# The third down-projection weight pair gets a place of its own and is loaded with the first two; the up stage's pools in another order

## The chip, the cores and the metric

The kernel is one program on one core of one Trainium2 chip. The metric is the device time of one execution in microseconds (us). A core has a matrix engine (TensorE, PE in the profile), a vector engine (DVE), a scalar engine (ACT), GpSimd (POOL) and SyncE (SP, which here only issues transfers). They run in parallel from their own instruction lists and wait for one another by semaphores. Operands lie in SBUF, an on-chip memory of 128 partitions; matmul results go to the eight banks of PSUM, and ACT and DVE carry them from there to SBUF.

## The reference

One inference step of a one-layer encoder trunk, all in float32: 1024 frames of a new stream and 64 frames of a running one (1088 rows), model width 1024.

```python
xn = rmsnorm(x, g)
proj = xn @ w_in                      # conv inputs B, C, h; q, k, v; two merge gates
ya = (B * causal_conv3(C * h)) @ w_cout
yb = band_attend(q, k, v, rel_bias) @ w_attn_out
x = x + (sigmoid(ga) * ya + sigmoid(gb) * yb) @ w_out
h = silu(xn2 @ w_ff1) * (xn2 @ w_ff3)  # xn2 = rmsnorm(x, g_ffn), inner width 2816
x = x + h @ w_ff2
y = rmsnorm(x, g_final)               # and the rolled caches
```

## The kernel before

**Arithmetic.** Each float32 operand is split into a high part (a rounded copy, a CAST by ACT, line 121) and a low part (the operand less the high part, a TENSOR_TENSOR by DVE, line 122). A product takes three matmuls: high by high, high by low, low by high. The large products are also done by Strassen-Winograd's scheme, in seven half-sized products for eight. They are always done in the order `STEPS = [1, 2, 6, 7, 5, 4, 3]`; steps 1, 2, 4 and 3 use quarters of the operands as they are, steps 6, 7 and 5 use sums of quarters.

**Stages**, by the profiled execution: norm, transposes and V (to 110 us), the rest of the input projection (to 340), gates and attention (to about 590), the merge of the two branches (`ya`, `yb`; to 692.6), the output product (`wo`, to 807, with the second norm's transposes between), the up stage and the down stage.

**The up stage** (to 1264.5) has 22 units of about 21 us, in pairs a0, b0 … a10, b10 (w_ff1 and w_ff3, 128 inner columns by two each). The moving operand of step p is the transposed activation, in a tile `mg` for steps 1, 2, 4, 3 and a tile `tt` for steps 6, 7, 5; the weights (`wha`, `whb`, `wla`, `wlb`) are stationary. A step is 24 matmuls of 272 columns. Results of the pair p go as `sa`, `sb` through SiLU and a product to `hq` buffers (three of them) and by a GpSimd-issued store to device memory (`h_d`), seven stores of 512 KB for each pair.

**The down stage** (1264.5 to 1506) multiplies by w_ff2. Its 22 rows of 128 are taken as 11 pairs `kp`, in four blocks of 2, 3, 3, 3 pairs. In a block, for each half g of the frames and each step p, PE does three matmuls for each pair and each of two frame tiles (12 in a row in the first block, 18 in a block of three; 132 for a step over the whole stage), with `ht` (read back from `h_d`) stationary and `ring` moving, 512 columns each. `ring1` to `ring7` hold the split weights, one tile for each step: `ring1`, `ring2`, `ring4`, `ring3` in the place of `mg`, `ring6`, `ring7`, `ring5` in the place of `tt` (pool `tpool`). PSUM results named A, B, D are copied (ACT, line 1518) or added (DVE, line 1520) to accumulators `acc`. After each block and half, the 64 running frames are done by `ys` matmuls.

The class `Down` stands for one pair: creating it loads its 1 MB of weights into a tile `w2r` (line 1304), and its seven `prep` steps split it into the rings (on DVE also subtractions, line 1319, in place or to `sf`). Tile `w2r` comes from `rpool`, two buffers of 8 KB per partition that nearly all weight loads of the kernel share (tag `raw`). So the load of pair kp waits until the last split of pair kp − 2 has read its buffer. Pairs 0 and 1 are created in the last up unit and prepared while it runs. Pairs 2, 3, 4 are created while block 0 runs:

```python
# last up unit, before
for kp in blocks[0]:
    W2[kp] = Down(kp)
ahead = [(W2[kp], {}) for kp in blocks[0]] + [(Refill(), {})]
...
# down stage, block b, half g: nk are the pairs of the next block
for n, kp in enumerate(nk):
    at = {0: 0, 1: 4 if first else 7, 2: 7}[n]
    for st in range(len(STEPS)):
        if (at + st) // 7 == g:
            todo.setdefault((at + st) % 7, []).append((kp, st))
    if at // 7 == g and at % 7 == 0:
        W2[kp] = Down(kp)
```

**What sets the order.** The program text fixes what depends on what; a scheduler then lists the instructions of each engine by its own estimates. So a load that is created elsewhere moves the splits and the copies around it on ACT and DVE. An instruction that waits holds all those behind it on its engine. The same scheduler decides where SP's loads stand.

**Where tiles lie.** Pools that are opened one after another are stacked in SBUF. Offsets in bytes per partition, from the sizes of the pools: scratch of the GpSimd-issued transfers 16384, constants 704, `rpool` 16384; so `tpool` starts at 33472, with `tt6`/`ring6` there, `tt7`/`ring7` at 50880, `tt5`/`ring5` at 68288. Each of these is a multiple of 64. `mg` and `ring1`, `ring2`, `ring4`, `ring3` start at 159712 and on, and `ht` and the stationary weights from 122848 on, each 32 above a multiple of 64. In the rows of the order below, a name ends with a running number, ours to tell tiles apart; the digits ahead of it are the pair, tile or frame.

Of the kernel before, what the change touches and what calls it, by code (L numbers as in the profile page):

```python
# [8 lines left out]
F32 = mybir.dt.float32  # L9
# [6 lines left out]
P = 128  # L16
D = 1024
# [47 lines left out]
def encoder_kernel(ctx: ExitStack, tc: tile.TileContext, ins, outs):  # L65
    nc = tc.nc
# [12 lines left out]
    rpool = ctx.enter_context(tc.tile_pool(name="rpool", bufs=2, reuse_waits="tile"))  # L79
# [94 lines left out]
    class Unit:  # L174
        def __init__(self, src, nm):
            self.nm = nm
            self.raw = rpool.tile([P, KD, 2 * P], F32, tag="raw", name=f"raw{nm}")
            nc.sync.dma_start(self.raw, src.rearrange("(k p) n -> p k n", p=P))
            self.w = {}
# [850 lines left out]
    pg_stack.close()  # L1030


    tpool = ctx.enter_context(tc.tile_pool(name="tpool", bufs=1, reuse_waits="tile"))
    up_stack = ExitStack()
    psA = up_stack.enter_context(tc.tile_pool(name="psA", bufs=2, space=PSUM, reuse_waits="tile"))
    hp0 = ctx.enter_context(tc.tile_pool(name="hp0", bufs=1, reuse_waits="tile"))

    tt = three_sums(tpool, "tt")
    ax = mg.t
# [247 lines left out]
    def refill():  # L1287

        while len(hts) < len(loads_h) and held[0] + len(loads_h[len(hts)][0]) <= 16:
            held[0] += len(loads_h[len(hts)][0])  # L1290
            h_load(*loads_h[len(hts)])
# [6 lines left out]
    class Down:  # L1298


        def __init__(self, kp):
            self.kp = kp
            self.raw = rpool.tile([P, 2, D], F32, tag="raw", name=f"w2r{kp}")
            nc.sync.dma_start(
                self.raw, ins["w_ff2"][0][2 * kp * P : 2 * (kp + 1) * P].rearrange("(r p) n -> p r n", p=P)
            )
            self.w = {}
# [58 lines left out]
    blocks = []  # L1366
# [3 lines left out]
    W2 = {}  # L1370

    def up_unit(n):
        l, p = names[n]
        return Unit(ins["w_ff1" if l == "a" else "w_ff3"][0][:, 2 * p * P : 2 * (p + 1) * P], f"{l}{p}")

    def up_run(n, unit, ahead):
        l, p = names[n]
        return run(unit, operands, bank2, snap2, (gate_done if l == "a" else hidden_done)(p), ahead)
# [26 lines left out]
    for n in range(1, len(names)):  # L1405
        if n + 1 < len(names):
            unit = up_unit(n + 1)
            ahead = [(unit, {2: (0, 1, 2)} if n == 1 else {})]
        else:
            for kp in blocks[0]:  # L1410
                W2[kp] = Down(kp)
            ahead = [(W2[kp], {}) for kp in blocks[0]] + [(Refill(), {})]
            refill()
        if n == 1:
            nxt += ahead
            r = r1
        else:
            r = up_run(n, this, ahead)
        for _ in r:
            pass  # L1420
        this = unit
# [8 lines left out]
    bufs = {(dp, "acc"): 1, (hp, "snap"): 3, (hp, "sa"): 4, (hp0, "snap"): 1, (hp0, "sa"): 1}  # L1430
    for n, (i, d) in enumerate(order):
        if n < len(homes):
            pool, tag = homes[n]
# [28 lines left out]
    for b, ks in enumerate(blocks):  # L1462
        first, final = b == 0, b == len(blocks) - 1
        nk = blocks[b + 1] if not final else []
        for g in range(2):
# [4 lines left out]
            for n, kp in enumerate(nk):  # L1470
                at = {0: 0, 1: 4 if first else 7, 2: 7}[n]
                for st in range(len(STEPS)):
                    if (at + st) // 7 == g:
                        todo.setdefault((at + st) % 7, []).append((kp, st))
                if at // 7 == g and at % 7 == 0:
                    W2[kp] = Down(kp)
            if final:
                xr = []
                for i in (2 * g, 2 * g + 1):
                    raw = rpool.tile([P, 2, D], F32, tag="raw", name=f"x1r{i}")  # L1480
# [13 lines left out]
            for si, js in turns:  # L1494
                p, ht = STEPS[si], hts[base + si]
                key = {1: "A", 6: "A", 5: "A", 3: "A", 2: "B", 7: "D", 4: "D"}[p]
                for j in js:
                    i = 2 * g + j
                    if (key, j) not in ps:
                        ps[key, j] = psD.tile(  # L1500
                            [P, 512], F32, tag="A" if key == "A" else "BD", name=f"{key}{b}_{i}",
                            bufs=2 if key == "A" else 4,
# [88 lines left out]
```

## Time and profile before

| | |
|---|---|
| time before | 1516.06 us, median of 3 runs (1512.9 to 1516.81) |
| span of the profiled execution, first to last instruction | 1513.8 us |
| PE busy | 1476.9 us, 98% of the span |
| DVE, ACT, POOL busy | 981.2 (65%), 682.7 (45%), 128.7 (9%) |
| granted TensorE clock | full in nearly every slice |
| PE between 1284.57 and 1295.9 (start of the down stage) | 4.95 us idle in four waits |
| tail after PE's last matmul | about 8 us |

The profiled execution's own time is known as this span; what lies around the span isn't given apart. The span stands 2.3 us below the median and inside the range of the three runs. In the rows of the profile a line's first number is the start in us, the second how long it is busy; brackets give the idle time ahead and what ended it.

### The profile page before, as it was taken

How to read it: one execution, taken by the hardware profiler on the slowest of the kernel's cores; microseconds unless marked ns; L12 is line 12 of the kernel's file. 1: busy time of each engine (PE TensorE's matmuls, PEld its weight loads, DVE VectorE, ACT ScalarE, POOL GpSimd, SP SyncE). 2: the span in 40 equal slices, each digit the busy share in tenths (PEclk: the TensorE clock that was granted, in tenths of full speed). 3: DMA queues.
4: the chain of work that ended last, by engine and by line, in shares of the span. 5: the costliest groups of instructions: out<-in, count | busy, mean ns of one | idle time of the engine just before them, and what ended most of it. 6: DMA issues, size and time to landing. Idle time of an engine off the chain costs nothing.

```text
span 1513.8 us, 26451 instructions
## 1 busy us (share of the span) xinstructions
PE 1476.9 (98%) x10178; PEld 1381.1 (91%) x10178; DVE 981.2 (65%) x1843; ACT 682.7 (45%) x1397; POOL 128.7 (9%) x236
## 2 busy tenths in 40 slices
PE   7999999999999999999999999999999999999997
PEld 5799999999999999998889999999999998788886
DVE  6886465642776752763489667666666668857576
ACT  6654433333776752542256444444444445402123
POOL 1210010001111121000100011100001011000000
PEclk9999999999999999999999999999999999999999
DMA  7597524168676529554432434443334449667675
GB/s 233 181 305 245 184 78 135 57 187 234 181 186 176 151 82 293 164 167 145 140 126 77 143 134 152 144 148 120 117 142 157 143 177 317 234 221 235 222 259 202
DMA packets 167518, 264.73 MB, mean 175 GB/s; under 512 B 19008, under 2 KB 103168, under 8 KB 167264
## 3 DMA queue, kind: packets, MB, share of 16 engines
q1 hardware_dynamic: 146736, 198.23, 42.2%
q0 software_dynamic: 19504, 62.71, 11.4%
q10 hardware_dynamic: 1152, 2.10, 0.4%
q8 instruction: 80, 1.31, 0.4%
q14 instruction: 46, 0.38, 0.1%
HBM read 171.06 MB, written 91.92 MB: 174 GB/s over the span
## 4 chain that ended last, share of the span: by engine, by line
PE 79%; DMA 8%; DVE 6%; ACT 3%; issue 3%; SPq 1%; POOL 0%; ACTq 0%; POOLq 0%; DVEq 0%
PE Aa L238 9%; PE Ab L238 9%; PE A L1508 7%; PE Da L238 4%; PE Db L238 4%; PE D L1508 3%; PE Bb L238 2%; PE Ba L238 2%; PE B L1508 2%; PE wo L1066 2%; PE wo L1068 2%; PE wo L1067 2%; PE t L903 2%; PE Ak L238 2%; PE g L300 2%
## 5 line engine op out<-in xcount | busy, mean ns | idle before, releaser
L1508 PE MATMUL A<-ring,ht 128*128 128x512 f32 x528 | 126.6, 393 | 3.6 <-ACT acc L1518 1.9
L1508 PEld LDWEIGHTS A<-ring,ht 128*128 128x128 f32 x528 | 98.8, 188 | 27.2 <-ACT acc L1518 3.2
L300 PE MATMUL g<-xn,whp 128*128 128x272 f32 x384 | 113.2, 295 | 0.0
L301 PE MATMUL g<-xn,whp 128*128 128x272 f32 x384 | 112.0, 292 | 0.0
L302 PE MATMUL g<-xn,wlp 128*128 128x272 f32 x384 | 111.6, 291 | 0.0
L121 ACT CAST ring<-w2r 128x512 fp32r<-128x512 f32 (+1 forms) x78 | 43.4, 587 | 105.7 <-PE A L1508 52.6
L121 ACT CAST hq<-sa 128x512 fp32r<-128x512 f32 x77 | 47.7, 619 | 86.4 <-DVE sa L1239 56.6
L814 DVE CUSTOM_DVE_ANT_0 p<-s,bb 128x640 f32<-128x640 f32 (+5 forms) x72 | 47.5, 661 | 45.5 <-DMA bb<-bias_d 28.6
L1227 POOL DMA_DIRECT2D h_d<-hq x77 | 40.9, 532 | 416.5 <-DVE hq L122 242.1
L122 DVE TENSOR_TENSOR hq<-sa,hq 128x512 fp32r<-128x512 f32 x77 | 53.1, 690 | 33.4 <-ACT hq L121 33.3
L300 PEld LDWEIGHTS g<-xn,whp 128*128 128x128 f32 x384 | 72.6, 189 | 1.0
L302 PEld LDWEIGHTS g<-xn,wlp 128*128 128x128 f32 x384 | 72.6, 189 | 0.5
L301 PEld LDWEIGHTS g<-xn,whp 128*128 128x128 f32 x384 | 72.7, 189 | 0.3
L1508 PE MATMUL D<-ring,ht 128*128 128x512 f32 x264 | 63.9, 393 | 1.3 <-ACT acc L1518 1.3
L122 DVE TENSOR_TENSOR wla<-rawa,wha 128x512 fp32r<-128x512 f32 x56 | 38.5, 687 | 40.5 <-ACT wha L121 40.5
L238 PE MATMUL Aa<-tt,wha 128*128 128x272 f32 x352 | 59.1, 289 | 2.5 <-ACT tt L121 2.5
L1508 PEld LDWEIGHTS D<-ring,ht 128*128 128x128 f32 x264 | 49.5, 188 | 13.1 <-ACT acc L1518 1.8
L122 DVE TENSOR_TENSOR ring<-w2r,ring 128x512 fp32r<-128x512 f32 (+1 forms) x78 | 49.0, 647 | 14.4 <-ACT ring L121 14.2
L238 PE MATMUL Ab<-mg,whb 128*128 128x272 f32 x352 | 58.4, 288 | 0.0
L238 PE MATMUL Aa<-mg,wha 128*128 128x272 f32 x352 | 58.3, 288 | 0.0
L238 PE MATMUL Ab<-tt,whb 128*128 128x272 f32 x352 | 58.2, 287 | 0.0
L121 ACT CAST wha<-rawa 128x512 fp32r<-128x512 f32 x56 | 34.8, 621 | 51.3 <-PE Ab L238 35.3
(519 smaller groups left out, 4368.2 us busy)
## 6 DMA issues: line engine op xcount, KB each, us to landing
h_d<-hq POOLq DMA_DIRECT2D x77, 512.0 KB, 3.5
ht<-h_d SPq DMA_DIRECT2D x154, 256.0 KB, 3.7
rawa<-in_w_ff SPq DMA_DIRECT2D x11, 1024.0 KB, 5.9
rawb<-in_w_ff SPq DMA_DIRECT2D x11, 1024.0 KB, 5.4
w2r<-in_w_ff SPq DMA_DIRECT2D x11, 1024.0 KB, 5.8
qd<-q_d SPq DMA_DIRECT2D x32, 272.0 KB, 4.7
rawp<-in_w_in SPq DMA_DIRECT2D x6, 1024.0 KB, 5.9
u_d<-scr SPq DMA_DIRECT2D x8, 544.0 KB, 4.6
```

Source lines behind the costliest of these rows:

```text
L121: act.copy(hi, src)
L122: vec.tensor_tensor(lo, src, hi.bitcast(F32), op=ALU.subtract)
L238: mm(t[:, j, :HN], w[:, k, :], x[p][:, l, k, j * HN : (j + 1) * HN], start=p in (1, 2, 7) and k == 0 and n == 0, stop=k == 3 and n == 2, s ...
L300: mm(out, a, p, start=k == 0, stop=False)
L301: mm(out, a, q, start=False, stop=False)
L302: mm(out, b, p, start=False, stop=k == kt - 1)
L814: vec.tensor_tensor_reduce(out=s if len(ps.shape) == 2 else s.rearrange("p (a b) -> p a b", a=2), in0=ps, in1=bias if len(ps.shape) == 2 e ...
L903: nc.tensor.transpose(tp[:, i * P : (i + 1) * P], s[:, i * P : (i + 1) * P], ident)
L1066: mm(ps, x(k, 0), wh, start=f, stop=False)
L1067: mm(ps, x(k, 0), wl, start=False, stop=False)
L1227: nc.gpsimd.dma_start(h_d[p, c - 1], hq.rearrange("p i l t -> p (i l t)").bitcast(F32))
L1508: mm(t, ht[k][:, j, x], w[:, l], start=p in (1, 2, 7) and k == 0 and n == 0, stop=k == len(ks) - 1 and n == 2, skip_group_check=p in (6, 5 ...
```

## The change

Three things are changed. The pool `hp0` and two new pools are opened ahead of `tpool`: `early`, with one 8 KB tile, and `lead`, with one tile of 32 bytes that nothing reads or writes. The raw weights of pair 2 lie in `early` instead of `rpool`, and pair 2 is created with pairs 0 and 1 in the last up unit. The scratch of GpSimd-issued transfers is set to 4096 bytes; 16384 was the default.

```diff
+    hp0 = ctx.enter_context(tc.tile_pool(name="hp0", bufs=1, reuse_waits="tile"))
+    early = ctx.enter_context(tc.tile_pool(name="early", bufs=1, reuse_waits="tile"))
+    lead = ctx.enter_context(tc.tile_pool(name="lead", bufs=1, reuse_waits="tile"))
+    lead.tile([P, 8], F32, name="lead")
     tpool = ctx.enter_context(tc.tile_pool(name="tpool", bufs=1, reuse_waits="tile"))
     up_stack = ExitStack()
     psA = up_stack.enter_context(tc.tile_pool(name="psA", bufs=2, space=PSUM, reuse_waits="tile"))
-    hp0 = ctx.enter_context(tc.tile_pool(name="hp0", bufs=1, reuse_waits="tile"))
...
-            self.raw = rpool.tile([P, 2, D], F32, tag="raw", name=f"w2r{kp}")
+            self.raw = (early if kp == blocks[1][0] else rpool).tile([P, 2, D], F32, tag="raw", name=f"w2r{kp}")
...
-            for kp in blocks[0]:
+            for kp in (*blocks[0], blocks[1][0]):
                 W2[kp] = Down(kp)
...
-                if at // 7 == g and at % 7 == 0:
+                if at // 7 == g and at % 7 == 0 and kp not in W2:
                     W2[kp] = Down(kp)
...
-    nc = bacc.Bacc("TRN2", target_bir_lowering=False, num_devices=1)
+    nc = bacc.Bacc("TRN2", target_bir_lowering=False, num_devices=1, dynamic_dma_scratch_size=4096)
```

By the sizes, the stack is now: scratch 4096, constants 704, `rpool` 16384, `hp0` 4352, `early` 8192 (at 25536), `lead` 32, and `tpool` from 33760: `ring6` 33760, `ring7` 51168, `ring5` 68576, each 32 above a multiple of 64. What lies below `tpool` has moved down by 12288, a multiple of 64; `mg`, `ht` and the weights stay where they were.

The number and the order of PE's matmuls are the same. Three lists show what moved elsewhere.

**SP, where the output product begins** (`ga` is the last gate tile of the merge, `wor` a quarter of w_out, `xr8` and `xr0` the residual inputs, `gb_row` the second norm's gain). Before:

```order
L965 DMA ga7_816_8079<-ga_d_87 128x272
L1047 DMA wor1_1_8552<-in_w_out 128x4x512
L1095 DMA gb_row_8239<-in_g_ffn 128x1024
L1102 DMA xr8_8278<-in_x_sample 64x512
L1102 DMA xr0_8302<-in_x_prompt 128x512
```

and now:

```order
L965 DMA ga7_816_8079<-ga_d_87 128x272
L1307 DMA w2r2_14190<-in_w_ff2 128x2x1024
L1098 DMA gb_row_8246<-in_g_ffn 128x1024
L1105 DMA xr8_8285<-in_x_sample 64x512
L1105 DMA xr0_8309<-in_x_prompt 128x512
L1050 DMA wor1_1_8559<-in_w_out 128x4x512
```

The load of pair 2, which stood among the first loads of the down stage, is now issued here, and the last quarter of w_out has gone behind the residual inputs. On DVE one subtraction for pair 2 (`w2r2` from `w2r2`) now stands between the last split of the merge (`ms`) and the addition to `xr8`.

**DVE, from the end of the up stage to the first accumulator additions** (`sa10` and `hq10` belong to the last up unit; `A0_0`, `B0_0` are PSUM results of block 0). Before:

```order
L1520 TENSOR_TENSOR acc1_0_14492<-B0_1_14537,acc1_0_14492 128x512
L122 TENSOR_TENSOR ring1_14214<-w2r2_14505,ring1_14214 128x512
L122 TENSOR_TENSOR ring2_14254<-w2r2_14505,ring2_14254 128x512
L122 TENSOR_TENSOR hq10_3_14462<-sa10_10_14141,hq10_3_14462 128x4x128
...
L122 TENSOR_TENSOR ring1_14214<-w2r3_14549,ring1_14214 128x512
L122 TENSOR_TENSOR ring4_14410<-w2r2_14505,ring4_14410 128x512
L1319 TENSOR_TENSOR w2r3_14549<-w2r3_14549 128x512
L122 TENSOR_TENSOR ring2_14254<-w2r3_14549,ring2_14254 128x512
L1319 TENSOR_TENSOR w2r2_14505<-w2r2_14505 128x512
L1319 TENSOR_TENSOR sf2_9046<-w2r3_14549 128x512
L1520 TENSOR_TENSOR acc4_1_14495<-A0_0_14507,acc4_1_14495 128x512
```

and now, from the first row of pair 3 on:

```order
L1322 TENSOR_TENSOR w2r3_14556<-w2r3_14556 128x512
L122 TENSOR_TENSOR ring1_14223<-w2r3_14556,ring1_14223 128x512
L122 TENSOR_TENSOR ring2_14263<-w2r3_14556,ring2_14263 128x512
L1322 TENSOR_TENSOR w2r2_14190<-w2r2_14190 128x512
L1322 TENSOR_TENSOR sf2_9053<-w2r3_14556 128x512
L122 TENSOR_TENSOR ring5_14379<-w2r3_14556,ring5_14379 128x512
L122 TENSOR_TENSOR ring4_14419<-w2r2_14190,ring7_14339 128x256
L122 TENSOR_TENSOR ring3_14484<-w2r2_14190,ring5_14379 128x256
L122 TENSOR_TENSOR ring6_14301<-sf2_9053,ring6_14301 128x512
L1322 TENSOR_TENSOR w2r3_14556<-sf2_9053,w2r3_14556 128x512
L1523 TENSOR_TENSOR acc4_1_14504<-A0_0_14514,acc4_1_14504 128x512
L1322 TENSOR_TENSOR w2r4_14697<-w2r4_14697 128x512
```

Four operations of pair 2 (the splits to `ring1`, `ring2`, `ring6` and a subtraction) have gone forward into the last up unit. The addition to `acc4_1` now stands behind ten operations from the first of pair 3, where it stood behind six.

**ACT, the same place.** Before, the copy of `D0_0` was followed by a cast of pair 3:

```order
L1518 COPY acc5_0_14494<-A0_1_14515 128x512
L121 CAST ring7_14330<-w2r2_14505 128x512
L1518 COPY acc4_1_14495<-D0_0_14586 128x512
L121 CAST ring1_14214<-w2r3_14549 128x512
L121 CAST ring4_14410<-w2r2_14505 128x512
L1518 COPY acc5_1_14496<-D0_1_14594 128x512
```

and now two casts of pair 3 stand ahead of that copy:

```order
L1521 COPY acc5_0_14503<-A0_1_14522 128x512
L121 CAST ring1_14223<-w2r3_14556 128x512
L121 CAST ring2_14263<-w2r3_14556 128x512
L1521 COPY acc4_1_14504<-D0_0_14593 128x512
L121 CAST ring5_14379<-w2r3_14556 128x512
L1521 COPY acc5_1_14505<-D0_1_14601 128x512
```

On SP, the load of pair 4 now stands right behind that of pair 3 at the start of the down stage; it stood some eight loads later.

## The prediction

> **What bounds the kernel now.** First the page: its head, part 1, then one group of part 5.
>
> ```profile
> span 1513.8 us, 26451 instructions
> PE 1476.9 (98%) x10178; PEld 1381.1 (91%) x10178; DVE 981.2 (65%) x1843; ACT 682.7 (45%) x1397; POOL 128.7 (9%) x236
> L1508 PE MATMUL A<-ring,ht 128*128 128x512 f32 x528 | 126.6, 393 | 3.6 <-ACT acc L1518 1.9
> ```
>
> PE is busy for 1476.9 of 1513.8 us, so it sets the time. The change leaves its instructions as they are; time can come only from its 36.9 us of idle time (1513.8 − 1476.9), or from how long a matmul takes. Which idle time the change can touch is read from the waits of PE (us in total, times, longest):
>
> ```profile
> PE xt L408 <- DVE scr L394: 9.7, 3, 8.2
> PE A L1508 <- ACT acc L1518: 1.9, 2, 1.3
> PE A L1508 <- DVE acc L1520: 1.7, 1, 1.7
> PE D L1508 <- ACT acc L1518: 1.3, 1, 1.3
> PE wo L1066 <- DVE xr L1088: 0.8, 1, 0.8
> ```
>
> The largest lies at the kernel's start, out of reach. Lines 1508 and 1066 are where the lists move: 1.9 + 1.7 + 1.3 = 4.9 us at the start of the down stage, and 0.8 where the output product begins. The first, in the timelines of PE, ACT, DVE and SP:
>
> ```profile
> 1285.92 1.66 PE L1508 MATMUL D<-ring,ht 128*128 128x512 f32 x6 [1.35 <-ACT acc L1518]
> 1289.25 3.03 PE L1508 MATMUL A<-ring,ht 128*128 128x512 f32 x12 [1.68 <-DVE acc L1520]
> 1292.86 1.66 PE L1508 MATMUL A<-ring,ht 128*128 128x512 f32 x6 [0.58 <-ACT acc L1518]
> 1295.86 1.64 PE L1508 MATMUL A<-ring,ht 128*128 128x512 f32 x6 [1.34 <-ACT acc L1518]
> ...
> 1274.61 1.66 ACT L121 CAST ring<-w2r 128x512 fp32r<-128x512 f32 x3 [3.31 <-DMA w2r<-in_w_ff]
> 1284.24 1.14 ACT L121 CAST ring<-w2r 128x512 fp32r<-128x512 f32 x2 [1.57 <-DMA w2r<-in_w_ff]
> 1285.29 0.58 ACT L1518 COPY acc<-D 128x512 f32<-128x512 f32 x1
> ...
> 1287.91 0.68 DVE L1319 TENSOR_TENSOR sf<-w2r 128x512 f32<-128x512 f32 x1
> 1288.51 0.68 DVE L1520 TENSOR_TENSOR acc<-A,acc 128x512 f32<-128x512 f32 x1
> 1289.12 0.75 DVE L122 TENSOR_TENSOR ring<-w2r,ring 128x256 fp32r<-128x256 f32 x2
> ...
> 1266.51 0.38 SPq L1304 DMA_DIRECT2D w2r<-in_w_ff  x1
> 1270.45 0.65 SPq L1304 DMA_DIRECT2D w2r<-in_w_ff  x1
> ```
>
> The load of pair 2 was issued at 1266.51 and ACT took it up at 1274.61, 8.1 us later. That of pair 3 was issued at 1270.45 and taken up at 1284.24, 13.8 us later. ACT stood before its cast for 1.57 us while a PSUM copy (1285.29) that PE needed stood behind it; and the addition at 1288.51, which frees a bank for A, stood on DVE behind the splits of both pairs. A late load holds ACT and DVE, and they hold PE.
>
> **The change part by part.**
>
> *Pair 2 out of the rush.* Its load leaves this place, and four of its DVE operations with it, 0.60 us each by the starts 1287.91 and 1288.51. They go into the last up unit, where the windows show no spare time on DVE (columns: sum, then PE, PEld, DVE, ACT, POOL, the clock, DMA share, GB/s):
>
> ```profile
> 1250.00:1255.00 5.00, 5.00 (x43) 5.00 (x42) 5.00 (x9) 3.02 (x7) 0.53 (x1) 1.00 0.77 240
> 1275.00:1280.00 5.00, 5.00 (x24) 4.02 (x23) 3.46 (x6) 3.00 (x6) 0.53 (x1) 1.00 1.03 415
> ```
>
> So the end of the up stage comes 4 × 0.60 = 2.4 us later on DVE. PE has its operands some way ahead there, and I charge nothing; without that cover it would wait up to 2.4 us. Pair 3 takes the buffer of pair 0, whose last split now stands some 12 rows later in DVE's list; its start before is 1265.80:
>
> ```profile
> 1265.80 0.68 DVE L122 TENSOR_TENSOR ring<-w2r,ring 128x512 fp32r<-128x512 f32 x1
> ```
>
> Nine of the rows are whole ones: 1265.80 + 9 × 0.60 = 1271.2, and the load goes out at about 1271.4. It is then the first of the two big loads, as pair 2 was, and I take that one's 8.1 us: landed at 1279.5. From there ten DVE operations stand ahead of the addition to `acc4_1`, eight whole ones and two halves (0.75 for both): 8 × 0.60 + 0.75 = 5.6, so the addition starts at 1285.1 and ends at 1285.8. PE, without the wait that ended at 1285.92, comes to A at 1289.25 − 1.68 − 1.35 = 1286.2. The first two waits go. The next, before 1292.86, is a copy by ACT that stands behind a cast of pair 3's last difference. On DVE that difference comes after the addition and four more operations: 1285.1 + 6 × 0.60 = 1288.7 at its end; with a cast and a copy, 0.58 each, the bank is free at 1289.9. PE wants it at 1286.2 + 2.9 = 1289.1 (12 matmuls, from 1289.25 to 1292.86 less 0.58, round 3). I leave 0.8 to 1.3 and take 1.3 of idle time in all, the last wait included. Gain 4.9 − 1.3 = **3.6**; ends 4.9 (all goes) and −1.6 (the load takes 13.8 us again: landed at 1285.2, addition ended at 1291.5, 5.3 us of waiting and 1.2 after it, 6.5 against 4.9). I am nearer to 3.6 since the bytes ahead of this load are fewer by pair 2's 1 MB.
>
> SP is held at the load of pair 4, which now stands behind pair 3's and waits for pair 1's buffer, two splits later, 1.2 us. Behind it wait `ht` tiles for steps that PE reaches some 25 us on: nothing. On DVE a first operation of pair 4 stands ahead of the addition to `acc5_1`. Issued at 1272.6 and 8.1 to 13.8 us on the way, it lands at 1280.7 to 1286.4; DVE is there at 1285.8. At most 0.6 us, inside the ends.
>
> *The start of the output product.* SP, chain and DVE:
>
> ```profile
> 694.71 0.38 SPq L1047 DMA_DIRECT2D wor<-in_w_out  x1
> ...
> 695.70 6.23 DMA xr<-in_x_sample
> ...
> 702.02 0.68 DVE L1088 TENSOR_TENSOR xr<-wo,xr 64x512 f32<-64x512 f32 x1 [6.88 <-DMA xr<-in_x_sample]
> ```
>
> The 64-row residual was asked for at 695.70, a microsecond behind 1 MB of w_out, and took 6.23 us; PE waited 0.77 us for the addition at 702.02. Now the w_out load goes behind it, and pair 2's load ahead of both goes out when the last `ya` matmul has read the buffer's old contents, near 687, so it has 8 us more to land. The residual comes early: gain **0.8**. DVE has one operation of pair 2 in front of the addition (0.68 us, in an idle 6.88). Had pair 2 not landed by then (13.8 after 687 is 700.8), PE would still get the bank at 700.8 + 1.4 = 702.2, before the 702.7 of now. Ends 0 and 0.8.
>
> *Where the rings lie.* The chain through block 1 (start, us, matmuls), and the up stage:
>
> ```profile
> 1322.34 4.08 PE B L1508 x18
> ...
> 1328.26 4.20 PE A L1508 x18
> 1332.46 4.20 PE D L1508 x18
> 1336.66 4.20 PE A L1508 x18
> 1340.86 4.11 PE D L1508 x18
> ...
> 1075.69 3.01 PE Ab L238 x24
> ...
> 1084.69 2.99 PE Db L238 x24
> ```
>
> In the order of steps 1, 2, 6, 7, 5, 4, 3, the row at 1322.34 is step 2, the three rows of 4.20 are steps 6, 7, 5, and the 4.11 is step 4. Same shapes, same `ht`; what differs is the moving tile: `ring6`, `ring7`, `ring5` in `tpool`, at multiples of 64 bytes, against 32 above them for the others. The added 32 bytes put all on the same footing. If the place is the cause, 3 × 132 = 396 matmuls (22 groups of 18) go from 4.20 to 4.08 or 4.11: 22 × 0.09 to 0.12 is 2.0 to 2.6. I take **2.5**, nearest to step 2's row; ends 0 and 2.6. In the up stage the sign is the other one: the `tt` steps (6, 7, 5) take 2.99 against 3.01 for `mg`. With `tt` on `mg`'s footing, 22 units × 3 steps × 0.02 = 1.3; since the difference is only two units of the last digit, I take a little less, a loss of **1.0**; ends 0 and 1.3.
>
> *DMA scratch of a quarter.* No row shows what it holds. The stores that need it, `h_d<-hq` in the fence below, are at most three at a time, as many as there are buffers, and I take 0; the upper end is the slower rival's. The rest (moved `hp0`, a shifted stack) costs nothing that a row shows.
>
> **Sum:** 3.6 + 0.8 + 2.5 − 1.0 = 5.9 us less. The profiled span would be 1513.8 − 5.9 = 1507.9. It stands 2.3 under the median of 1516.1, so the median would be **1510.2**, 0.39% less. A measurement of this kernel tells about 0.3%, 4.5 us, from no change.
>
> **The rivals.**
>
> *The place does not matter.* Steps 6, 7, 5 would differ for a reason of their own, both up and down, and terms three and four fall: 3.6 + 0.8 = 4.4, time 1511.7, within 0.3%. For it: in the up stage the same tiles are the faster ones. Against it: the seven steps are the same instructions on other tiles. The Trainium skill, "SBUF — State Buffer", section "Who interferes with whom", gives PE two read ports, one for the moving operand and one for the weights, and says that it never waits on anyone. By that the place of a tile would change nothing, and the sum would be 4.4; the rows 4.20 and 4.08 speak against it. Chance 0.16.
>
> *Pair 3's load is as late as before.* The windows above show DMA full (1.03, 415 GB/s) in 1275 to 1280; two big loads are still issued within 2 us of one another. The first term is then −1.6 and the sum 0.7 less: 1515.4. Chance 0.13.
>
> *Slower: the small scratch lets only one store at a time go.* The stores of one pair, GpSimd's timeline, and how long one takes to land:
>
> ```profile
> 1223.69 0.53 POOL L1227 DMA_DIRECT2D h_d<-hq  x1 [2.81 <-DVE hq L122]
> 1225.73 0.54 POOL L1256 DMA_DIRECT2D hs_d<-hs  x1 [1.51 <-DVE hs L122]
> 1227.05 0.53 POOL L1227 DMA_DIRECT2D h_d<-hq  x1 [0.78 <-DVE hq L122]
> 1228.25 0.53 POOL L1227 DMA_DIRECT2D h_d<-hq  x1 [0.67 <-DVE hq L122]
> ...
> 1233.25 0.53 POOL L1227 DMA_DIRECT2D h_d<-hq  x1 [2.51 <-DVE hq L122]
> ...
> h_d<-hq POOLq DMA_DIRECT2D x77, 512.0 KB, 3.5
> ```
>
> A store takes 0.53 + 3.5 = 4.0 us. Now up to three are under way. One at a time from 1223.69, the third (1227.05) would land at 1235.7. Its buffer is wanted by the store at 1233.25, the third `hq` after it, whose cast and split (0.6 each) start near 1232. ACT would be held for 3.7 us in each of 11 pairs, with PE's evacuations behind it: 41 us, or 8 if a step of 3.0 hides most each time; I take the middle, 25. 1510.2 + 25 = 1535. It decides as soon as the scratch cannot hold the descriptors of two 512 KB stores. Against it: POOL is at 9%, and what is asked of it at once is little. The Trainium skill, "DMA: Bandwidth & Descriptors", section "SWDGE vs HWDGE vs iDMA", says that GpSimd writes the descriptors into rings in a reserved part of SBUF; it gives no price, and no run here shows a full ring. Chance 0.13.
>
> **How the numbers follow.** The forecast has the rest, 0.58, and is faster by over 0.3%. The first two rivals are within it: 0.16 + 0.13 = 0.29. Slower is the last, 0.13. Low end: all ends at their best, 4.9 + 0.8 + 2.6 − 0 = 8.3, 1507.8, less 2.3 for the spread of the runs: 1505.5. High end: the late load, 1515.4, and some 1.6 for the spread: 1517. The slower rival stays outside.
>
> **What would show it.** PE's waits at line 1508 down to about 1.3 us and the one at line 1066 gone; a `w2r` load near 687; the cast of pair 3 taken up by about 1280; steps 6, 7, 5 at 4.08 to 4.11 for 18 matmuls, and the `tt` steps at 3.01 for 24. Wrong would be: 4.20 still there (the place is not the cause); new waits of PE between 1262 and 1275 (DVE had no room for pair 2's splits); waits of ACT's `hq` casts on `h_d` stores grown by several us a pair (the scratch).

## The result, and the profile after

The changed kernel takes 1508.59 us (median of 20 runs, 1502.49 to 1513.56), the kernel before 1514.75 us (20 runs beside it, 1510.70 to 1519.65). The ratio is 0.9963, 95% interval 0.9951 to 0.9974: 0.37% less, where 0.39% was forecast (1510.2 us).

First the page after (head and part 1) and PE's waits at line 1511, which was line 1508:

```profile
span 1511.6 us, 26449 instructions
PE 1476.0 (98%) x10178; PEld 1384.2 (92%) x10178; DVE 981.3 (65%) x1843; ACT 683.1 (45%) x1397; POOL 128.8 (9%) x236
...
PE A L1511 <- ACT acc L1521: 1.1, 1, 1.1
PE A L1511 <- DVE acc L1523: 0.8, 1, 0.8
```

The spans differ by only 2.2 us, and that is the first thing to learn here: a span of one execution is no measure of a change this small. The attention stages ahead of the change scatter: over the profiles of this document the output product begins between 690.41 and 696.96 us. In this profile it begins at 696.58 us, in the one before at 692.60, with nothing changed ahead of it but what lies where. The stages behind are steadier. Taken from the timeline of PE (start of the first matmul of one stage to that of the next, for the last one to PE's last matmul):

| stage | before | after | difference |
|---|---|---|---|
| output product | 103.59 | 102.77 | −0.82 |
| up stage | 468.15 | 469.68 | +1.53 |
| down stage | 241.50 | 234.58 | −6.92 |
| sum | 813.24 | 807.03 | −6.21 |

The up stage is counted from its first matmul, which comes before the second norm's last transposes. The sum, 6.2 us less, agrees with the medians (1514.75 − 1508.59 = 6.16; by the interval of the ratio 3.9 to 7.4). Now the lines that answer to those of the prediction. The start of the down stage, in the timelines of PE, DVE and SP:

```profile
1269.03 2.21 PE L1511 MATMUL A<-ring,ht 128*128 128x512 f32 x9
1290.82 3.01 PE L1511 MATMUL A<-ring,ht 128*128 128x512 f32 x12 [0.78 <-DVE acc L1523]
1294.96 3.02 PE L1511 MATMUL A<-ring,ht 128*128 128x512 f32 x12 [1.12 <-ACT acc L1521]
...
1284.60 0.68 DVE L1322 TENSOR_TENSOR w2r<-w2r 128x512 f32<-128x512 f32 x1
1290.09 0.68 DVE L1523 TENSOR_TENSOR acc<-A,acc 128x512 f32<-128x512 f32 x1
...
1276.00 3.32 SPq L1307 DMA_DIRECT2D w2r<-in_w_ff  x2
```

Four waits have become two, 4.95 us have become 1.90. (In the ten profiles of this document that have pair 2 in `early`, these waits sum to 1.4 to 3.0 us. The two with the old order and the rings in their old places have 4.95 and 5.05.) The loads of pairs 3 and 4 stand in one group on SP (x2). Then the chain of what ended last, in block 1:

```profile
1322.50 4.08 PE B L1511 x18
...
1328.43 4.08 PE A L1511 x18
1332.52 4.08 PE D L1511 x18
1336.60 4.08 PE A L1511 x18
1340.68 4.08 PE D L1511 x18
```

Steps 6, 7 and 5 (the three rows from 1328.43) take 4.08 us as step 2 does; they took 4.20. At the output product, SP and DVE:

```profile
690.77 0.38 SPq L1307 DMA_DIRECT2D w2r<-in_w_ff  x1
699.84 0.48 SPq L1105 DMA_DIRECT2D xr<-in_x_sample  x1
701.00 0.42 SPq L1050 DMA_DIRECT2D wor<-in_w_out  x1
...
702.64 0.68 DVE L1091 TENSOR_TENSOR xr<-wo,xr 64x512 f32<-64x512 f32 x1 [2.23 <-DMA xr<-in_x_sample]
```

The residual is asked for ahead of the last quarter of w_out and is there 2.8 us later; it took 6.2. PE's wait of 0.77 us is gone. In the up stage, the chain of a second profile of the same changed kernel shows steps 6 and 7 of one unit at 3.01 (2.99 before):

```profile
1084.00 3.01 PE Ab L238 x24
1087.00 3.01 PE Db L238 x24
```

### The profile page after: what moved, and what is told of

It reads as the page before. It is cut to its first block, busy times and chain, and to the rows that moved or that the text cites. A ratio compares the mean times of both kernels' runs of the same rounds, so it can differ in the third digit from the quotient of the medians.

```text
span 1511.6 us, 26449 instructions
## 1 busy us (share of the span) xinstructions
PE 1476.0 (98%) x10178; PEld 1384.2 (92%) x10178; DVE 981.3 (65%) x1843; ACT 683.1 (45%) x1397; POOL 128.8 (9%) x236
## 4 chain that ended last, share of the span: by engine, by line
issue 43%; PE 43%; DVE 4%; POOL 4%; DMA 3%; ACT 1%; POOLq 0%; ACTq 0%; SPq 0%; DVEq 0%
PE A L1511 7%; PE D L1511 3%; POOL h_d L1230 2%; PE g L300 2%; PE g L301 2%; PE g L302 2%; PE B L1511 2%; PE t L903 2%; PE pv L928 2%; PE Ak L238 2%; PE Acc L238 2%; PE Acb L238 2%; PE Agb L238 2%; PE Ach L238 2%; PE s L856 1%
```

## The experiments

All ratios are to the kernel before, run beside them. Stage times are taken from each kernel's one profile as in the table above. "ns" below is the mean time from one matmul's start to the next, from the trace, without matmuls behind a wait or at half clock; remainders are those of a tile's address, in bytes per partition, divided by 256.

**The parts alone.** The change without the 32 bytes:

```diff
-    lead = ctx.enter_context(tc.tile_pool(name="lead", bufs=1, reuse_waits="tile"))
-    lead.tile([P, 8], F32, name="lead")
```

> The change without the 32 bytes: pair 2 is loaded early, the scratch is small, but tpool starts at a multiple of 64 as before. Theory (two separate causes: the early load ends waits, the place of the rings speeds the matmuls): the down stage, from its first matmul to PE's last, takes 238.4 us (241.5 before, less the 3.05 us of waits that went; 234.6 in the changed kernel), with steps 6, 7, 5 at 4.20 us for 18 matmuls; the up stage 468.2 (before 468.15, changed 469.7); the whole 3.9 us less than before (3.05 and 0.8 at the output product), ratio 0.9975. Rival (the place of a tile is nothing to PE; the steps got faster because DMA and the other engines were less in the way): down stage 234.6, steps 6, 7, 5 at 4.08, ratio 0.996.

Ratio 0.9970 (0.9955 to 0.9985); down stage 237.75 us, up stage 468.34. The chain of block 1:

```profile
1326.50 4.20 PE A L1509 x18
1330.70 4.20 PE D L1509 x18
1334.90 4.20 PE A L1509 x18
```

Waits of the down stage as in the changed kernel (0.91 and 1.11 us), matmuls as before. The early load is one cause, worth 3.75 us of the down stage (241.50 − 237.75), and it costs the up stage nothing. The other 3.17 us of the down stage (237.75 − 234.58) go with the 32 bytes, and so do 1.34 us lost in the up stage. The output product gained nothing here: the wait at the residual is gone, but PE waits 1.10 us for the last split of `ms`. That wait, of 0.2 to 1.3 us, comes and goes among the profiles, with the early load and without it.

The kernel before with the 32 bytes alone:

```diff
+    lead = ctx.enter_context(tc.tile_pool(name="lead", bufs=1, reuse_waits="tile"))
+    lead.tile([P, 8], F32, name="lead")
     tpool = ctx.enter_context(tc.tile_pool(name="tpool", bufs=1, reuse_waits="tile"))
```

> The kernel before with the 32 bytes alone: no early load, scratch as it was. Theory: down stage 237.6 us (241.5 less 3.9), steps 6, 7, 5 at 4.08 for 18, the waits at its start 4.9 as before; up stage 469.7 (tt steps at 3.01 for 24); the wait of 0.8 us at the output product stays; the whole 2.4 us less, ratio 0.9984. Rival (the place is nothing): as before in every stage, 241.5 and 468.2, ratio 1.000.

Ratio 0.9999 (0.9984 to 1.0013), down stage 240.03, up stage 470.63. Steps 6, 7, 5 are at 4.08 as expected, and yet the down stage gained 1.5 and not 3.9. The timeline of PE and the windows (sum, PE, PEld, DVE, ACT, POOL, granted clock, DMA share, GB/s) say where it went:

```profile
1289.22 2.08 PE L1510 MATMUL D<-ring,ht 128*128 128x512 f32 x6 [2.51 <-ACT acc L1520]
1292.56 7.82 PE L1510 MATMUL A<-ring,ht 128*128 128x512 f32 x22 [1.25 <-DVE acc L1522]
...
1288.00:1290.00 2.00, 0.78 (x3) 0.67 (x4) 1.80 (x3) 2.00 (x5) 0.00 (x0) 1.00 1.07 392
1292.00:1294.00 2.00, 1.44 (x3) 1.17 (x4) 2.00 (x5) 0.56 (x2) 0.00 (x0) 0.50 0.02 4
1294.00:1296.00 2.00, 2.00 (x6) 1.61 (x5) 2.00 (x4) 0.99 (x2) 0.00 (x0) 0.50 0.82 215
```

About 1 us after the wait of 2.51 us, and before that of 1.25, the granted clock fell to 0.50 for some 7 us (1290.2 to 1297.1), and eleven matmuls went at 427 ns instead of 227, 11 × 0.2 = 2.2 us. The sum fits: waits 1.0 less, rings 2.6 less, clock 2.2 more is 1.4 less; measured 1.5. So the 32 bytes alone do what was expected of the rings, and in this profile the lost clock took most of it back. Over the 12 runs the time shows no gain, where a ratio of 0.9984 was expected. One profile does not tell whether the others lost their clock too; but even with a full clock some 3 us less in the down stage and 1.3 more in the up stage leave about 0.1%, which this interval can't tell from nothing. The rival (the place is nothing) falls by the 4.08.

The kernel before with the small scratch alone:

```diff
-    nc = bacc.Bacc("TRN2", target_bir_lowering=False, num_devices=1)
+    nc = bacc.Bacc("TRN2", target_bir_lowering=False, num_devices=1, dynamic_dma_scratch_size=4096)
```

> The kernel before with a scratch of 4096 bytes alone; everything on the left of SBUF moves down by 12288 bytes. Theory (the scratch costs nothing): as before, down stage 241.5, up stage 468.2, waits of ACT's hq casts on the stores of h_d about 16 us in all, ratio 1.000. Rival (a small scratch holds up GpSimd's stores and cost the change a part of its gain): these waits grow to over 20 us, the up stage is 0.5 us or more longer, ratio above 1.000.

Ratio 1.0006 (0.9989 to 1.0022); up stage 467.49, down stage 241.66. ACT's waits for the stores, in the kernel before and here:

```profile
ACT hq L121 <- DMA h_d<-hq: 16.2, 12, 2.5
...
ACT hq L121 <- DMA h_d<-hq: 18.9, 14, 3.1
```

They grow by 2.7 us in all, over 11 pairs. PE waits once more than before, where a store held ACT longest:

```profile
981.43 0.62 ACT L121 CAST hq<-sa 128x512 fp32r<-128x512 f32 x1 [3.13 <-DMA h_d<-hq]
...
985.76 0.77 PE L238 MATMUL Aa<-tt,wha 128*128 128x272 f32 x4 [0.51 <-ACT sa_Q L226]
```

ACT's copy of a PSUM result (`sa_Q`) came late behind the cast, and PE waited for it. The up stage is none the longer for it only because this profile has no stretch at half clock at its start (last section), which the one before has. So the slower rival of the prediction is out: it wanted 3.7 us in each pair. But that the scratch costs nothing is not shown. The two profiles with 16384 bytes have 16.2 and 16.4 us of these waits of ACT, the twelve with 4096 bytes 17.4 to 22.5, and the interval leaves room for some 3 us.

**What the place of a tile does.** The 32 bytes help the rings and cost the `tt` tiles, so one version gives each its own: the tiles of `tpool` are made longer, `tt` begins at the start and `ring` 32 bytes behind.

```diff
-    lead.tile([P, 8], F32, name="lead")
...
+        p: tpool.tile([P, 8 * HT + 16], F32R, tag=f"o{p}", name=f"tt{p}")[:, : 8 * HT].rearrange(...)
...
+                ring[p] = pool.tile([P, 8 * HT + 16], F32R, tag=f"o{p}", name=f"ring{p}")[:, 8 : 8 + 8 * HT]
```

> The change without the 32 bytes ahead; instead the three tiles of tpool are 64 bytes longer, tt starts at the tile's start (a multiple of 64) and ring 32 bytes behind it. Theory (in the up stage the moving operand is faster at a multiple of 64, in the down stage 32 above): down stage 234.6 us as in the changed kernel, up stage 468.2 as before (1.5 less than the changed kernel), the whole 7.7 us less than before, ratio 0.995. Rival 1 (the up stage grew by 1.5 us because DVE and ACT have pair 2's splits in it): up stage 469.7, ratio 0.996. Rival 2 (the place is nothing): all as the changed kernel, ratio 0.996.

Ratio 0.9967 (0.9952 to 0.9982); up stage 467.60, but down stage 237.76 instead of 234.6. The up stage looks as hoped and isn't: this profile, too, has no stretch at half clock at its start, which is worth 1.4 us against the profile before. Its `tt` matmuls take 124.9 ns, half-way between 124.5 before and 125.3 in the changed kernel. Steps 6, 7 and 5 in block 1:

```profile
1324.71 4.10 PE A L1516 x18
1328.81 4.14 PE D L1516 x18
1332.95 4.19 PE A L1516 x18
```

Three rings, all 32 above a multiple of 64, and three times. The longer tiles had put them at remainders 224, 32 and 96 by 256 (and `tt` at 192, 0 and 64); so 64 was not the number that counts. This miss was the most useful run. Two runs went through the other remainders, with tiles 256 bytes longer: 0, 64 and 128 for `ring6`, `ring7`, `ring5` in the first (the offsets below are in floats), 96, 160 and 32 in the second.

```diff
+                c = {6: 16, 7: 32, 5: 48}[p]
+                ring[p] = pool.tile([P, 8 * HT + 64], F32R, tag=f"o{p}", name=f"ring{p}")[:, c : c + 8 * HT]
```

> The changed kernel without the 32 bytes; tt stays at 192 in terms of the remainder of the address by 256, and ring6, ring7, ring5 are put at remainders 0, 64 and 128 (in the changed kernel 224, like the other rings and ht; before 192). Start-to-start times of the matmuls so far: 226.8 ns at 224, 229.9 at 32, 232.6 at 96, 233.4 at 192. Theory (what counts is the remainder by 256, not that by 64): three different times between 226 and 236 ns, 0 near 229, 64 near 231, 128 near 233. Rival (only the remainder by 64 counts, and the differences in the run with tt and ring apart came from something else): all three alike, near 233.4 as at 192, 4.20 us for 18.

> As the run with remainders 0, 64, 128, now ring6 at 96, ring7 at 160, ring5 at 32. Theory (the place and not the step counts): ring6 at 232.6 ns, as ring5 had at 96; ring5 at 229.9, as ring7 had at 32; ring7 between 232 and 235. Rival (the steps differ by themselves): ring5 slowest again at 232.6, ring6 fastest.

The chains of block 1, remainders 0, 64, 128, then 96, 160, 32:

```profile
1326.95 4.20 PE A L1516 x18
1331.15 4.21 PE D L1516 x18
1335.36 4.20 PE A L1516 x18
```

```profile
1326.91 4.19 PE A L1516 x18
1331.10 4.19 PE D L1516 x18
1335.30 4.12 PE A L1516 x18
```

In ns: 233.2 at 0, 233.2 at 64, 233.9 at 128, 233.0 at 96 and at 160, 229.5 at 32; before, 233.3 to 233.5 at 192; changed, 226.8 at 224. So `ring5` is fast at 224, half-way at 32, slow at 128 and 192: the place counts, not the step. My graded guesses for 0, 64 and 128 were wrong: 224 alone is fast, 32 lies between, and all the rest is slow. And 224 is just where `ht`, the stationary operand, lies. Does the ring's place count, or its distance from `ht`? One run moved `ht` (and the up stage's weights) to 192 and left all rings at 224:

```diff
+    shift = ctx.enter_context(tc.tile_pool(name="shift", bufs=1, reuse_waits="tile", side="right"))
+    shift.tile([P, 8], F32, name="shift")
     ws = ctx.enter_context(tc.tile_pool(name="ws", bufs=8, reuse_waits="tile", side="right"))
```

> The changed kernel with 32 bytes put ahead of the pool of the stationary operands: ht and the up stage's weights move from remainder 224 by 256 to 192, all rings stay at 224. Theory 1 (the distance between moving and stationary operand counts): all seven steps of the down stage change alike, to about what a ring at 0 takes against ht at 224 (near 229 ns, 4.13 us for 18, the down stage some 2 us longer than 234.6). Theory 2 (the moving operand's place alone counts): 226.8 ns and 4.08 us in all seven steps, down stage 234.6 as in the changed kernel.

Steps 2, 6 and 4 in block 1:

```profile
1320.85 4.19 PE B L1513 x18
1326.89 4.20 PE A L1513 x18
1339.50 4.20 PE D L1513 x18
```

All seven steps are slow now (233.1 to 233.5 ns), the down stage 240.21 us. The ring's place alone is out. What was left is that `ht` at 192 might be slow in itself. The last of these runs has the same `shift` but no `lead`, so `ring6`, `ring7`, `ring5` and `ht` are all at 192 and the other rings at 224:

> The changed kernel without its 32 bytes, but with 32 bytes ahead of the pool of the stationary operands: ring6, ring7, ring5 and ht all at remainder 192 by 256, ring1, ring2, ring4, ring3 at 224. Theory 1 (moving and stationary operand must have the same remainder): the picture is turned over, steps 6, 7, 5 at 226.8 ns (4.08 us for 18) and steps 1, 2, 4, 3 at 233.5 (4.20); down stage 234.6 + 528 x 6.7 ns = 238.1. Theory 2 (ht at 192 is slow in itself, whatever the ring's place): all seven steps at 233.5, down stage 240.2 as in the run with ht alone moved.

```profile
1324.36 4.19 PE B L1511 x18
1330.40 4.11 PE A L1511 x18
1334.50 4.08 PE D L1511 x18
1338.58 4.08 PE A L1511 x18
1342.66 4.20 PE D L1511 x18
```

The picture is turned over: steps 7 and 5 at 4.08, step 6 close to it, steps 2 and 4 slow; 226.9 to 228.2 ns against 233.3 to 233.5; down stage 238.52, 238.1 expected. Step 6 has 4.11 since its first five matmuls, behind a slow step, still take 228 to 236 ns; step 4 had 4.11 before for the same reason and has 4.08 in the changed kernel. A matmul of 512 columns goes at 227 ns when moving and stationary operand have the same remainder by 256, and at 233 at nearly every other distance that was tried (230 at a distance of 64). That 256 is the number, and not 128 or 512, is shown too: at a distance of 128 (`ring6` at 96) it is slow, and in the next version the remainders by 512 of `ring7` and `ht` differ by 256 and it is fast (226.7).

**The version with both.** `tt` stays at 192, where the up stage was faster, and the three rings are put at 224, 32 bytes into tiles that are 256 bytes longer. It was run twice, beside other kernels, and the changed kernel was run again:

> The changed kernel without the 32 bytes ahead; tt of the up stage at remainder 192 by 256 as before, ring6, ring7, ring5 at 224 as in the changed kernel. Theory (each stage has its own best place): steps 6, 7, 5 of the down stage at 226.8 ns, 4.08 us for 18, down stage about 234.7 us; tt steps of the up stage at 124.7 ns as before instead of 125.4, which is 1.1 us less than in the changed kernel; the whole 1.1 us under the changed kernel, ratio to before 0.9955. Rival (the up stage's difference is not from the place): up stage as in the changed kernel, ratio 0.9963.

> The changed kernel itself, for a comparison beside the versions with tt and rings apart. Ratio to before 0.9963; down stage 234.6 us, tt steps at 125.4 ns.

> The version with tt at 192 and the rings at 224 again. Ratio to before 0.9955, 1.1 us under the changed kernel beside it; down stage 234.7 us, tt steps at 124.6 ns.

| kernel | ratio | interval | up stage | down stage |
|---|---|---|---|---|
| changed | 0.9963 | 0.9951 to 0.9974 | 469.68 | 234.58 |
| changed, again | 0.9956 | 0.9940 to 0.9972 | 471.87 | 235.93 |
| both places | 0.9951 | 0.9933 to 0.9970 | 468.17 | 234.69 |
| both places, again | 0.9952 | 0.9937 to 0.9967 | 468.19 | 235.02 |

The `tt` matmuls take 124.5 ns against 125.3 in both pairs of profiles, 1.3 us over the stage's 1584, with the down stage kept. (The 471.87 has besides a wait of 0.94 us behind a late store, and twice as long a stretch at half clock.) The intervals overlap: by the measured times alone it is not shown to be faster than the changed kernel.

**Is it the early load or only the way out of the rush?** Pair 2 has no place of its own; the pool of all raw loads has three buffers (tiles as in the version with both places):

```diff
-    rpool = ctx.enter_context(tc.tile_pool(name="rpool", bufs=2, reuse_waits="tile"))
+    rpool = ctx.enter_context(tc.tile_pool(name="rpool", bufs=3, reuse_waits="tile"))
...
-            self.raw = (early if kp == blocks[1][0] else rpool).tile([P, 2, D], F32, tag="raw", name=f"w2r{kp}")
+            self.raw = rpool.tile([P, 2, D], F32, tag="raw", name=f"w2r{kp}")
```

> As the run with tt at 192 and the rings at 224, but pair 2 has no place of its own: the pool of all raw weight loads has three buffers instead of two (the same room). The lists at the start of the down stage are as in the changed kernel; the load of pair 2 goes out behind those of pairs 0 and 1 in the last up units instead of at the output product. Theory (it is enough that the load is out of the rush at the start of the down stage): waits there 1.9 us, down stage 234.7, up stage 468.2; the output product without the wait of 0.77 only if its last weights, which now have a third buffer, go out earlier than the residual. Rival (the load must be done long before): its 1 MB in the last units holds up pairs 0 and 1 or ht, new waits of PE of 1 us or more near 1262 to 1280. Ratio to before 0.995 to 0.996 by the first, 0.997 by the second.

Ratio 0.9971 (0.9956 to 0.9985); up stage 468.65, down stage 235.02. Pair 2 was asked for at 1244.99, some 22 us ahead of the down stage, and that was enough: no wait of PE arose near 1262 to 1280. So the time is the rival's 0.997, but not by the rival's mechanism. What it lost lies at the output product (107.27 us instead of 102.77), on SP and in PE's waits:

```profile
695.09 0.38 SPq L178 DMA_DIRECT2D rawa<-in_w_ff  x1
696.15 0.48 SPq L1105 DMA_DIRECT2D xr<-in_x_sample  x1
...
PE wo L1069 <- DVE xr L1091: 1.9, 1, 1.9
```

With a third buffer the first load of w_ff1 goes out just ahead of the residual, and PE's wait is back, 1.9 us long. Behind it the granted clock was at half from 704.4 to 707.9, some 1.6 us more, and the wait for `ms` took 0.7. So the second term of the prediction is a matter of what 1 MB load stands ahead of a small one. A program with the place of its own but with pair 2 created at the old point was not run, for nothing differs in it: the lists of all engines come out the same, row for row. The scheduler puts the load where its buffer is free, and the line that asks for it earlier does nothing.

## Why the prediction was right

*Pair 2 out of the rush* (forecast 3.6, measured 3.05 of waits, 3.75 in the run without the 32 bytes). Counted from the first matmul of the down stage, the steps came out closely. Pair 3's load: forecast 1271.4 − 1264.34 = 7.1, measured 1276.00 − 1269.03 = 7.0. DVE at pair 3's first operation: 15.2 and 15.6. The addition: 20.8 and 21.1. The copy by ACT: a wait of 0.8 to 1.3, measured 1.12. The step that failed is "PE comes to A at 1286.2", 21.9 after the start: it came at 21.0 (1290.82 − 0.78 − 1269.03), since the slow rings of block 0 had gone (0.26 us), and with the waits some matmuls beside them that had taken 0.1 us and more longer. So the second wait went from 1.68 to 0.78 and not to nothing. (The sum also has 2.9 us for the 12 matmuls behind it, where its own row gives 3.0.) No wait of PE arose at the end of the up stage: the 2.4 us of DVE work had its cover.

*The output product* (0.8): measured 0.82. The wait at the residual is gone in all ten profiles with the load in `early`, by the mechanism named; the run with three buffers showed it from the other side. That the whole stage agrees to the digit is luck: it takes 102.5 to 104.6 us in these ten, as the wait for `ms` comes and goes.

*Where the rings lie* (2.5): right in size and sign, wrong in the rule. From 4.20 to 4.08 in 22 groups of 18 is 2.6 us; by the mean time of a matmul (6.6 ns less, 396 times) it is 2.6 too. But not the multiple of 64 decides: it is whether the ring has the remainder by 256 of `ht`. That the added 32 bytes hit the one value that works was luck: the forecast could not have told it from 32 above any other multiple of 64. The rest of the 6.92 us, some 1.3, is not in the forecast's terms: 0.2 at step 4 (its first five matmuls), 0.2 at the `ys` matmuls, which are also faster with the 32 bytes alone, and 0.8 at matmuls beside the old waits, which take 0.1 to 0.2 longer each.

*The up stage* (a loss of 1.0): measured 1.3 by the `tt` matmuls (0.8 ns, 1584 times), 1.5 by the stage. Most of the rest is `mg`'s step 4 behind a `tt` step, 125.3 ns where it had 124.9. Why `tt` does better at 192 is open. Its slices start 1088 bytes apart (272 columns of 4 bytes), so they take four remainders by 256 in turn, and the down stage's rule can't be carried over.

*The scratch* (0): no cost shown in the time (ratio 1.0006, 0.9989 to 1.0022), but ACT's waits for the stores are longer in every profile that has it, so nothing at all isn't shown either.

The sum came out closer than its terms: more was won by the rings and what hangs on them than forecast, and more was lost in the up stage.

The three rivals fall. The place matters, by the runs that moved only places: 226.8 against 233 ns with nothing changed but addresses. The Trainium skill, "SBUF — State Buffer", section "Who interferes with whom", gives PE's two read ports as independent and says that PE never waits on anyone. That section is about engines that hold up one another and names no price of an address; the step from it to "the place of a tile would change nothing" does not hold here to the last 3%. Whether this is a wait at a port or something else in the fetch is open. Pair 3's load was not late, and the stores did not go one at a time.

## What to carry to other kernels

Where PE is busy for 98% of the time, compare groups of the same instruction on different tiles: 4.20 against 4.08 in the chain was nearly half of what there was to win. Then vary the one suspect over all its values and also move its partner; that is how "32 above a multiple of 64" became "the same remainder by 256 as the stationary operand". And read a change of a third of a per cent by stages: the spans differed by 2.2 us where the change is worth 6.

## What the runs showed of the hardware

A matmul of 512 columns of 4 bytes took 226.8 ns from start to start with moving and stationary operand at the same remainder by 256, 229.5 to 229.9 with the moving one 64 ahead, and 232.6 to 233.9 at the other distances in steps of 32. After a change from a slow pair of tiles to a fast one, the first five matmuls were still slow.

A short idle time of PE can cost more than itself. At the start of the up stage every profile has waits of 1.38 and 1.12 us with one matmul between; in the changed kernel's windows the granted clock then reads:

```profile
814.00:816.00 2.00, 2.00 (x10) 2.00 (x10) 2.00 (x5) 0.83 (x2) 0.00 (x0) 0.50 0.03 8
```

In 11 of 14 profiles 13 to 25 matmuls went at 227 ns instead of 125, 1.3 to 2.6 us. In the other three (the small scratch alone, the 64 bytes longer tiles, `ht` moved with the rings at 224) hardly one did after the same two waits, so a stage time compares only between profiles that agree in this. The Trainium skill, "TensorE: Matmul & The Clock Gate", Part 1 ("The HAM clock gate"), says that the clock goes to half after an idle window of about 3.4 us, counted by a free-running window. The 0.50 and the 427 ns agree, and the stretches at half clock are 3.4 or 6.8 us long; but here 2.5 us of idle time, broken by a matmul, was often enough. At the start of the down stage one of the three profiles with the old waits lost 2.2 us in this way, and none of the eleven with pair 2 loaded ahead. That may make the removed waits worth a little more, on average, than their own length; three profiles are too few to show it.
